# A streaming encoder step: an early end of the gating stage for tile 0, the last two chunks of the last tile alone, and conditioning pieces that wait by an account

## The chip, the core and the metric

One core of a Trainium2 chip runs the kernel. TensorE (PE in the profile) multiplies, VectorE (DVE) and ScalarE (ACT) do what is elementwise, SyncE (SP) issues the DMAs, and each engine works through its own queue in order. The metric is the device time in microseconds of one execution; the time before is the median of three.

## The reference

One step of an encoder of two layers, for a prompt of 1024 frames and 32 frames of a running stream, with shared weights. Everything is float32.

```python
for i in range(DEPTH):                                       # DEPTH = 2
    mod = silu(c) @ w_ada[i] + b_ada[i]                      # 1024 x 6144, c one vector per request group
    sh1, sc1, gt1, sh2, sc2, gt2 = split(mod, 6)
    h = rmsnorm(x, g_norm[i, 0]) * (1 + sc1) + sh1
    mix = sgu_mixer(h, ...) if i == 0 else pool_mixer(h, ...)
    x = x + gt1 * rmsnorm(mix, g_norm[i, 1])
    h = rmsnorm(x, g_norm[i, 2]) * (1 + sc2) + sh2
    f = square(relu(h @ ffn_w_up[i])) @ ffn_w_down[i]        # 1024 x 4096, 4096 x 1024
    x = x + gt2 * rmsnorm(f, g_norm[i, 3])

def sgu_mixer(h, ...):
    u, v = split(gelu(h @ w_in), 2)                          # 1024 x 4096
    v = rmsnorm(v, g_v)
    s[g] = (w_s[g] * mask) @ v[chunk, g] + b_s[g]            # 8 groups of 256 channels, chunks of 128 frames
    return (u * s) @ w_out, v                                # 2048 x 1024
```

The outputs are x of both requests, the normalised v rows of the stream, and the last 15 rows that the pooling mixer saw.

## The kernel before

**Tiles.** The 1056 frames lie along the free dimension in three tiles: 384, 384, and 288 (256 of the prompt and the 32 of the stream). The channels lie on the partitions, as 8 blocks of 128. Each tile has an accumulator `acc[t]` in SBUF.

**Products.** A product in float32 is made of three in the fast format: high part by high, low by high, and high by low (lines 771 to 773; 798 to 800 for v). Activations are split once, and each 512 KB piece of a weight is split when it arrives: ACT copies its high part (`wh`, line 367), DVE subtracts it for the low one (`wl`).

**The stream.** All weights come in one list, `stream`, in the order in which they are to be used: the weights of the gating stage ("v", "u", "o"), of the channel MLP ("up", "dn"), and between them the pieces of the conditioning matrix `w_ada` ("ada"), put in by `some_ada(n)`. Loads are issued on SP in this order, as many as there are slots, and consumed in this order by `stream_step`. `weave` calls it after every group of products; `need_w` and `need_ada` call it until the wanted item has been reached, so whatever stands ahead of it in the list is worked off at that point.

**Conditioning.** A column block of `w_ada` comes in two loads. `do_ada` multiplies it by the conditioning vector on DVE, 16 operations into the one buffer `aa`. A fold on PE then sums over the partitions (`ada`, line 453, 8 small products). Every fourth block, ACT copies the sums to `adas`, and a transpose on PE (`adat`, line 469) and a few DVE operations make `mod` and `coef` of them. Folds are put in the list `deferred`, and `run_deferred` runs all of them at the next step.

**Order of the work.** `sgu_item(gs, t, ...)` does two groups of the gating stage for one tile: four u products with gelu, two gates (`psp`), and, behind the next item's first product, the output product `po`. The loop goes over the pairs of groups (0,1), (2,3), (4,5), (6,7), and in each over the three tiles. With the last pair, `Stat` sums the squares of a tile (`sq_rs_t`), and `mix_to_ffn` for that tile goes into `fillers`: norm (`pn_rs`), residual, second norm (`r1_0_t`), and the MLP's operand `hh`, `hl`. The MLP of a layer goes by `passes`: (layer, chunk of 512 hidden channels, tiles). In layer 0, chunks 0, 1 and 4 to 7 take the tiles one by one, each with its own load of the weights, and chunks 2 and 3 all three at once. In layer 1 it is chunks 0 to 3 one by one and 4 to 7 with all three.

`time` is an account that is kept while the program is built: an estimate of how far PE and DVE have come. `weave` pulls steps of `fillers` while the account of DVE is behind that of PE.

**The end.** For the last tile, the last norm is taken row by row: the accumulator is scaled (`scale_last`) and transposed (`turn_last`, line 1146) while the last product still runs. `last` sums the squares by 6 small products (`pn_last`), takes the reciprocal root `r_last`, and 6 DVE operations (`xlast`) make the rows that go out. The other tiles go out by `residual`, 24 transposes (`yT`, line 1405), copies on ACT and one store per 128 frames (line 1407). Tile 1's 24 stand behind the last product of the program.

Of the kernel before, what the change touches and what calls it, by code (L numbers as in the profile page):

```python
# [9 lines left out]
F32 = mybir.dt.float32  # L10
# [24 lines left out]
def tile_stream_encoder_step(  # L35
# [87 lines left out]
    eps1 = const.tile([P, 1], F32, name="eps1")  # L123
    nc.vector.memset(eps1, EPS)
# [125 lines left out]
    def w_groups(gs):  # L250
        for g in gs:
            for k in range(2):
                f = 2 * g + k
                add_w(
                    ("u", g, k),
# [3 lines left out]
        for q in range(2):  # L259
            for g in gs:  # L260
                add_w(
                    ("o", g, q),
# [31 lines left out]
    passes += [(1, c, every) for c in range(4, 8)]  # L294
# [26 lines left out]
    groups = [(g, g + 1) for g in range(0, 8, 2)]  # L321
    for i, gs in enumerate(groups):
        w_groups(gs)
        if i < 3:
            some_ada((6, 8, 8)[i])
    wide = [n for n, (l, _, tiles) in enumerate(passes) if len(tiles) > 1]
    for n in range(len(passes)):
        w_chunk(n)
        if n in wide:
            some_ada(12 if passes[n][0] == 0 else 2)  # L330
# [7 lines left out]
    state = {"issued": 0, "next": 0, "raw": 0}  # L338
# [55 lines left out]
    def do_ada_pe(l, sl, q, r):  # L394
# [31 lines left out]
        deferred.append(fold)  # L426


    def do_ada(l, sl, q, r):
# [16 lines left out]
        def fold():  # L446
# [29 lines left out]
            deferred.append(fold2)  # L476

        deferred.append(fold)

    def run_deferred():  # L480
        for _ in range(len(deferred)):
            deferred.pop(0)()
# [34 lines left out]
    def stream_step():  # L517
# [4 lines left out]
        run_deferred()  # L522
# [11 lines left out]

    def need_w(key):
        while key not in witem:
            assert stream_ready(), key
            stream_step()
        return witem[key]

    def need_ada(l, which):
# [4 lines left out]
        run_deferred()  # L546
        run_deferred()
# [37 lines left out]
    def weave(streams=1):  # L585
        if streams:
            n = 0
            run_deferred()
            while n < streams and stream_ready():
                stream_step()  # L590
                n += 1
# [30 lines left out]
    class Stat:  # L622

        def __init__(self, t, tag, split=True):
            self.t, self.tag, self.n, self.split = t, tag, ncol[t], split

        def square(self, k, src=None):
# [11 lines left out]
            if w == 1:  # L641
                for j in [k - 1] if k < 7 else [6, 7]:
                    if j > 0:
# [314 lines left out]
    def sgu_item(gs, t, mix, after):  # L958
# [26 lines left out]
        def up(g, k):  # L985
# [3 lines left out]
            products(ps, n, up_terms(("u", g, k), t))  # L989
            if t == NT - 1:  # L990
                w_finish(("u", g, k))
# [53 lines left out]
        def down():  # L1045
            for d in range(KB):
                ps = ps_dn(f"po{gs[0]}_{t}_{d}")
                terms = []
                for j, (a, b) in enumerate(hid):
                    wh, wl = need_w(("o", gs[j // 2], d // 4))  # L1050
# [8 lines left out]
                if t == NT - 1 and d % 4 == 3:  # L1059
                    for g in gs:  # L1060
                        w_finish(("o", g, d // 4))
# [13 lines left out]
    def ffn_item(p, t, after):  # L1075
# [17 lines left out]
        def down():  # L1093
            for d in range(KB):
# [11 lines left out]
                if after is not None:  # L1106
                    st.square(d)
                    if l == 1 and t == NT - 1:
                        scale_last(d)
                        if d > 0:  # L1110
# [65 lines left out]
    for gs in groups:  # L1176
        mix = {g: sgu_group(g) for g in gs}
        for t in range(NT):
            sgu_item(gs, t, mix, to_ffn0 if gs == groups[-1] else None)
# [166 lines left out]
    def to_out(st):  # L1346
# [8 lines left out]
        def last():  # L1355

            turn_last(KB - 1)
# [101 lines left out]
```

## Time and profile before

| what | us |
| --- | --- |
| time, median of 3 runs | 2229.41 (2227.93 to 2232.3) |
| the profiled execution | 2227.71 |
| its span | 2225.9 |
| PE busy | 2191.3 (98%) |
| DVE busy | 1370.2 (62%) |
| ACT busy | 950.1 (43%) |
| mean granted clock of PE | 0.995 |

The span is the time between the first and the last recorded instruction. Matmuls are pipelined, so the duration of one is longer than the distance to the next. The granted clock is the share of PE's full speed that the throttle allowed in a stretch.

### The profile page before, as it was taken

The page shows a single profiled execution, that of the slowest core. Times are in us where ns is not written, and L with a number is a line of the kernel's source. Part 1 is how long each engine was busy: PE and PEld are TensorE (multiplying, and loading weights), DVE is VectorE, ACT ScalarE, POOL GpSimd, SP SyncE. Part 2 cuts the span into 40 slices and gives each one's busy share as a digit, 9 for nine tenths or more (in the row PEclk, how much of TensorE's full clock was granted, in tenths as well). Part 3 has the DMA queues.
Part 4 walks back from the last instruction along what each step waited for, and adds up shares of the span by engine and source line. Part 5 has one row for each costly group of instructions (what it writes and reads, how often), then busy time and mean ns, then how long its engine had stood idle before and what let it go on. Part 6 is the DMA issues. An engine that isn't in the chain of part 4 may idle for free.

```text
span 2225.9 us, 33634 instructions
## 1 busy us (share of the span) xinstructions
PE 2191.3 (98%) x13478; PEld 2096.9 (94%) x13478; DVE 1370.2 (62%) x2609; ACT 950.1 (43%) x1641; POOL 0.7 (0%) x6
## 2 busy tenths in 40 slices
PE   7999999999999999999999999999999999999998
PEld 4777899999998999999999999999999999999998
DVE  4855746575478856675447878878775553424355
ACT  4633422112256654223435556666564542312334
POOL 0000000000000000000000000000000000000000
PEclk9999999999999999999999999999999999999999
DMA  8465624233145544333444556655454541202112
GB/s 291 158 220 166 194 73 136 84 123 94 56 137 157 175 140 142 95 123 114 131 130 136 167 156 192 189 186 159 144 172 128 159 152 48 86 15 81 57 51 94
DMA packets 344897, 295.67 MB, mean 133 GB/s; under 512 B 10179, under 2 KB 322955, under 8 KB 344741
## 3 DMA queue, kind: packets, MB, share of 16 engines
q1 hardware_dynamic: 344468, 293.43, 42.3%
q8 instruction: 105, 1.72, 0.3%
q14 instruction: 52, 0.42, 0.1%
q10 hardware_dynamic: 272, 0.10, 0.0%
HBM read 261.65 MB, written 31.84 MB: 132 GB/s over the span
## 4 chain that ended last, share of the span: by engine, by line
PE 86%; DMA 1%; ACT 0%; DVE 0%; issue 0%; DVEq 0%; SPq 0%; ACTq 0%
PE pf L771 11%; PE pf L772 11%; PE pf L773 11%; PE pg L771 11%; PE pg L772 11%; PE pg L773 11%; PE po L771 3%; PE po L772 3%; PE po L773 3%; PE pu L771 2%; PE pu L773 2%; PE pu L772 2%; PE psp L1005 1%; PE pp L1322 1%; PE ada L453 0%; PE yT L1405 0%
## 5 line engine op out<-in xcount | busy, mean ns | idle before, releaser
L771 PE MATMUL pf<-hh,wh_up 128*128 128x384 f32 (+1 forms) x1536 | 497.8, 325 | 2.2 <-ACT hh L745 1.8
L771 PE MATMUL pg<-fh,wh_dn 128*128 128x384 f32 (+1 forms) x1536 | 498.4, 325 | 0.0
L772 PE MATMUL pf<-hl,wh_up 128*128 128x384 f32 (+1 forms) x1536 | 496.5, 324 | 0.0
L773 PE MATMUL pf<-hh,wl_up 128*128 128x384 f32 (+1 forms) x1536 | 495.3, 323 | 0.0
L772 PE MATMUL pg<-fl,wh_dn 128*128 128x384 f32 (+1 forms) x1536 | 494.8, 322 | 0.0
L773 PE MATMUL pg<-fh,wl_dn 128*128 128x384 f32 (+1 forms) x1536 | 493.9, 322 | 0.0
L771 PEld LDWEIGHTS pf<-hh,wh_up 128*128 128x128 f32 x1536 | 288.6, 188 | 5.7 <-ACT hh L745 2.2
L771 PEld LDWEIGHTS pg<-fh,wh_dn 128*128 128x128 f32 x1536 | 288.5, 188 | 2.9 <-issue 1.2
L772 PEld LDWEIGHTS pf<-hl,wh_up 128*128 128x128 f32 x1536 | 288.7, 188 | 1.2 <-DVE hl L79 0.7
L772 PEld LDWEIGHTS pg<-fl,wh_dn 128*128 128x128 f32 x1536 | 288.6, 188 | 0.8
L773 PEld LDWEIGHTS pg<-fh,wl_dn 128*128 128x128 f32 x1536 | 288.7, 188 | 0.0
L773 PEld LDWEIGHTS pf<-hh,wl_up 128*128 128x128 f32 x1536 | 288.7, 188 | 0.0
L79 DVE TENSOR_TENSOR wl_up<-raw,wh_up 128x1024 fp32r<-128x1024 f32 x144 | 176.1, 1223 | 167.3 <-ACT wh_up L367 167.0
L367 ACT ACTIVATE wh_up<-raw 128x1024 fp32r<-128x1024 f32 x144 | 152.7, 1060 | 286.0 <-PE pf L772 233.4
L79 DVE TENSOR_TENSOR acc<-acc,pg 128x384 f32<-128x384 f32 (+1 forms) x336 | 173.7, 517 | 159.9 <-PE pg L773 159.3
L367 ACT ACTIVATE wh_dn<-raw 128x1024 fp32r<-128x1024 f32 x144 | 152.5, 1060 | 202.7 <-PE pg L772 169.4
L79 DVE SCALAR_TENSOR_TENSOR aa<-raw,csil,aa 128x256 f32<-128x256 f32 x560 | 231.0, 477 | 1.9 <-DMA raw<-in_w_ada_dram 1.9
L79 DVE TENSOR_TENSOR wl_dn<-raw,wh_dn 128x1024 fp32r<-128x1024 f32 x144 | 176.0, 1223 | 81.7 <-ACT wh_dn L367 81.6
L1087 ACT ACTIVATE r<-pf 128x384 f32<-128x384 f32 (+1 forms) x192 | 86.6, 452 | 216.3 <-PE pf L773 211.5
L79 DVE TENSOR_TENSOR fl<-r,fh 128x384 fp32r<-128x384 f32 (+1 forms) x192 | 100.2, 522 | 117.0 <-ACT fh L925 115.4
L771 PE MATMUL pu<-hh,wh_u 128*128 128x384 f32 (+1 forms) x384 | 126.5, 329 | 0.0
L773 PE MATMUL pu<-hh,wl_u 128*128 128x384 f32 (+1 forms) x384 | 124.5, 324 | 0.0
(254 smaller groups left out, 2881.5 us busy)
## 6 DMA issues: line engine op xcount, KB each, us to landing
raw<-in_ffn_w_up_dram SPq DMA_DIRECT2D x144, 512.0 KB, 4.1
raw<-in_ffn_w_down_dram SPq DMA_DIRECT2D x144, 512.0 KB, 3.4
raw<-in_w_ada_dram SPq DMA_DIRECT2D x96, 512.0 KB, 3.9
raw<-in_sgu_w_in_dram SPq DMA_DIRECT2D x32, 512.0 KB, 4.6
xd<-acc SPq DMA_DIRECT2D x8, 1536.0 KB, 7.2
xo_r<-xd SPq DMA_DIRECT2D x32, 384.0 KB, 4.0
vd<-vt SPq DMA_DIRECT2D x32, 256.0 KB, 2.9
raw<-in_sgu_w_out_dram SPq DMA_DIRECT2D x16, 512.0 KB, 3.9
```

What stands on the lines that cost most here:

```text
L79: return op(out, *args, **kw)
L367: act(out=wh, in_=r, func=AF.Copy)
L771: mm(ps[:, :n], wh, rh, start=i == 0, stop=False)
L772: mm(ps[:, :n], wh, rl, start=False, stop=False)
L773: mm(ps[:, :n], wl, rh, start=False, stop=i == last)
L1005: mm(sp[:, c * P : (c + 1) * P], vl[:, c, k * P : (k + 1) * P], wr[:, c * P : (c + 1) * P], start=True, stop=True,)
L1087: act(out=r[:, :n], in_=ps[:, :n], func=AF.Relu)
L1322: mm(ps[:, :n], wg[:, k, e * P : (e + 1) * P], A(t, 2 * g + k), start=k == 0, stop=k == 1)
```

## The change

Three things are changed, and some arithmetic at the end.

- The gating stage goes over `mixes`: the pairs (0,1) and (2,3) for all tiles, (4,5) and (6,7) for tile 0 alone, then (4,5) and (6,7) for tiles 1 and 2. The weights and the spatial matrices of groups 4 to 7 are loaded, split and transposed twice. The numbers of conditioning pieces between the weights are changed with it.
- In layer 1, chunks 6 and 7 run for tiles 0 and 1, and after that for tile 2 alone, with loads and splits of their own.
- `stream_waits` holds `weave` back from the next item of the stream: a weight, if it is more than five ahead of the last one used and DVE's account is over 1 us ahead of PE's; a conditioning piece, if DVE's account is over 0.5 us ahead, or if the fold before it hasn't run. A deferred step can have a time on PE's account before which it isn't run: 0.3 us after the chain for a fold, 0.8 us after the copy for its transpose. `need_w` and `need_ada` go on as before.
- At the end, epsilon is added with the first addition of squares. The sum over the channel blocks is finished by PE, which adds the last block's squares to those of the other seven; `ms_last` is gone. `turn_last` goes two blocks at a time.

```diff
@@ -120,8 +120,6 @@
-    eps1 = const.tile([P, 1], F32, name="eps1")
-    nc.vector.memset(eps1, EPS)
@@ -247,19 +245,20 @@
         for q in range(4):
             add_w(*v_item(p, q))
 
-    def w_groups(gs):
+    def w_groups(n):
+        gs, _ = mixes[n]
         for g in gs:
             for k in range(2):
                 f = 2 * g + k
                 add_w(
-                    ("u", g, k),
+                    ("u", n, g, k),
                     sgu_w_in[0][:, f * P : (f + 1) * P].rearrange("(k p) f -> p k f", p=P),
                     (8, P),
                 )
         for q in range(2):
             for g in gs:
                 add_w(
-                    ("o", g, q),
+                    ("o", n, g, q),
                     sgu_w_out[0][g * 256 : (g + 1) * 256, q * 512 : (q + 1) * 512].rearrange(
                         "(k p) d -> p k d", p=P
                     ),
@@ -291,7 +290,10 @@
     passes += [(0, c, every) for c in range(2, 4)]
     passes += [(0, c, [t]) for t in every for c in range(4, 8)]
     passes += [(1, c, [t]) for t in every for c in range(4)]
-    passes += [(1, c, every) for c in range(4, 8)]
+    passes += [(1, c, every) for c in range(4, 6)]
+
+    passes += [(1, c, every[:-1]) for c in (6, 7)]
+    passes += [(1, c, [NT - 1]) for c in (6, 7)]
 
     rest = []
 
@@ -318,16 +320,19 @@
         w_vpiece(p)
         some_ada(8)
     rest += [(1, j) for j in (*range(8, 16), *range(8), *range(16, 48))]
-    groups = [(g, g + 1) for g in range(0, 8, 2)]
-    for i, gs in enumerate(groups):
-        w_groups(gs)
-        if i < 3:
-            some_ada((6, 8, 8)[i])
-    wide = [n for n, (l, _, tiles) in enumerate(passes) if len(tiles) > 1]
-    for n in range(len(passes)):
+
+    mixes = [((0, 1), every), ((2, 3), every), ((4, 5), every[:1]), ((6, 7), every[:1])]
+    mixes += [((4, 5), every[1:]), ((6, 7), every[1:])]
+    for n in range(len(mixes)):
+        w_groups(n)
+        if n < 2:
+            some_ada((6, 8)[n])
+    for n, (l, c, tiles) in enumerate(passes):
         w_chunk(n)
-        if n in wide:
-            some_ada(12 if passes[n][0] == 0 else 2)
+        if l == 0:
+            some_ada(12 if len(tiles) > 1 else 4 if c in (4, 5) and tiles == every[:1] else 0)
+        elif len(tiles) > 1:
+            some_ada(4)
     some_ada(99)
 
     worder = [s[1] for s in stream if s[0] == "w"]
@@ -335,7 +340,7 @@
     wdone = set()
     raws = {}
     loads = {}
-    state = {"issued": 0, "next": 0, "raw": 0}
+    state = {"issued": 0, "next": 0, "raw": 0, "used": 0}
     deferred = []
 
     def in_raw(k):
@@ -423,7 +428,7 @@
             )
             ada_finish(l, sl, red.rearrange("p (s h m) -> p s h m", s=1, h=2))
 
-        deferred.append(fold)
+        defer(fold)
 
 
     def do_ada(l, sl, q, r):
@@ -473,13 +478,20 @@
                     pb[:, :P].rearrange("p (v h m) -> p m h v", v=NV, h=2)[:, 0:4],
                 )
 
-            deferred.append(fold2)
-
-        deferred.append(fold)
-
-    def run_deferred():
-        for _ in range(len(deferred)):
-            deferred.pop(0)()
+            defer(fold2, 0.8)
+
+        defer(fold, 0.3)
+
+    def defer(step, us=None):
+
+        at = 0.0 if us is None else max(time["pe"], time["dve"]) + us
+        deferred.append((at, step))
+
+    def run_deferred(force=False):
+        n = len(deferred)
+        while n > 0 and (force or deferred[0][0] <= time["pe"]):
+            deferred.pop(0)[1]()
+            n -= 1
 
     junk = room("l", NT - 1, "xsq")
 
@@ -519,7 +531,7 @@
         k = state["next"]
         kind, key, ap, shape = stream[k]
         issue()
-        run_deferred()
+        run_deferred(force=kind == "ada" and key[2] == 0)
         r = raws.pop(k)
         if kind == "w":
             do_w(key, r)
@@ -532,7 +544,17 @@
             state["raw"] -= 1
         issue()
 
+    def stream_waits():
+
+        kind, key = stream[state["next"]][:2]
+        if kind == "w":
+            return bool(fillers) and wpos[key] > state["used"] + 5 and time["dve"] > time["pe"] + 1.0
+        if kind == "ada" and deferred and key[2] == 0:
+            return True
+        return kind == "ada" and time["dve"] > time["pe"] + 0.5
+
     def need_w(key):
+        state["used"] = max(state["used"], wpos[key])
         while key not in witem:
             assert stream_ready(), key
             stream_step()
@@ -543,8 +565,8 @@
         while state["next"] <= k:
             assert stream_ready()
             stream_step()
-        run_deferred()
-        run_deferred()
+        run_deferred(True)
+        run_deferred(True)
 
     def w_finish(key):
         wdone.add(key)
@@ -586,7 +608,7 @@
         if streams:
             n = 0
             run_deferred()
-            while n < streams and stream_ready():
+            while n < streams and stream_ready() and not stream_waits():
                 stream_step()
                 n += 1
         while time["dve"] < time["pe"] and fillers:
@@ -639,8 +662,17 @@
             )
 
             if w == 1:
-                for j in [k - 1] if k < 7 else [6, 7]:
-                    if j > 0:
+                for j in [k - 1] if k < 7 else [6, 7] if self.split else [6]:
+                    if j == 1 and not self.split:
+                        stt(
+                            out=sq[:, 0, :],
+                            in0=sq[:, 0, :],
+                            scalar=epsT,
+                            in1=sq[:, j, :],
+                            op0=ALU.add,
+                            op1=ALU.add,
+                        )
+                    elif j > 0:
                         tt(out=sq[:, 0, :], in0=sq[:, 0, :], in1=sq[:, j, :], op=ALU.add)
             else:
                 for j in [k - 2] if k < 6 else [4, 6]:
@@ -955,7 +987,9 @@
         nc.vector.memset(wt[64:P, 0:64], 0.0)
         return wt, bb
 
-    def sgu_item(gs, t, mix, after):
+    def sgu_item(p, t, mix, after):
+        gs, tiles = mixes[p]
+        last = t == tiles[-1]
         n = ncol[t]
         col0, npr, nsm = TILES[t]
         nch = npr // P
@@ -986,9 +1020,9 @@
             if k == 0:
                 inputs(g)
             ps = ps_up(f"pu{g}_{t}_{k}")
-            products(ps, n, up_terms(("u", g, k), t))
-            if t == NT - 1:
-                w_finish(("u", g, k))
+            products(ps, n, up_terms(("u", p, g, k), t))
+            if last:
+                w_finish(("u", p, g, k))
             u = t_m(f"u{g}_{t}_{k}")
             act(out=u[:, :n], in_=ps[:, :n], func=AF.Gelu_apprx_tanh)
             us.append(u)
@@ -1047,7 +1081,7 @@
                 ps = ps_dn(f"po{gs[0]}_{t}_{d}")
                 terms = []
                 for j, (a, b) in enumerate(hid):
-                    wh, wl = need_w(("o", gs[j // 2], d // 4))
+                    wh, wl = need_w(("o", p, gs[j // 2], d // 4))
                     o = (j % 2) * 512 + (d % 4) * P
                     terms.append((wh[:, o : o + P], wl[:, o : o + P], a[:, :n], b[:, :n]))
                 products(ps, n, terms)
@@ -1056,9 +1090,9 @@
                     st = Stat(t, f"rs_{t}")
                 if after is not None:
                     st.square(d)
-                if t == NT - 1 and d % 4 == 3:
+                if last and d % 4 == 3:
                     for g in gs:
-                        w_finish(("o", g, d // 4))
+                        w_finish(("o", p, g, d // 4))
                 weave(d % 2)
             if after is not None:
                 after(st)
@@ -1107,7 +1141,8 @@
                     st.square(d)
                     if l == 1 and t == NT - 1:
                         scale_last(d)
-                        if d > 0:
+                        if d in (2, 4, 6):
+                            turn_last(d - 2)
                             turn_last(d - 1)
                 if last and d % 2 == 1:
                     w_finish(("dn", p, d // 2))
@@ -1173,10 +1208,10 @@
     def to_ffn0(st):
         fillers.append((f"ffn0_{st.t}", mix_to_ffn(st, 0)))
 
-    for gs in groups:
+    for p, (gs, tiles) in enumerate(mixes):
         mix = {g: sgu_group(g) for g in gs}
-        for t in range(NT):
-            sgu_item(gs, t, mix, to_ffn0 if gs == groups[-1] else None)
+        for t in tiles:
+            sgu_item(p, t, mix, to_ffn0 if gs[-1] == 7 else None)
 
     sgu_stack.close()
     late = pool("late")
@@ -1354,23 +1389,26 @@
 
         def last():
 
-            turn_last(KB - 1)
+            turn_last(KB - 2)
             pn = ps_dn("pn_last")
             nb = len(LAST)
-            for i, (c0, _, _) in enumerate(LAST):
-                mm(
-                    pn[:, 2 * i : 2 * i + 2],
-                    st.sq[:, 0, c0 : c0 + P],
-                    ones[:, 0:2],
-                    start=True,
-                    stop=True,
-                )
+            for k in (0, KB - 1):
+                if k > 0:
+                    turn_last(KB - 1)
+                for i, (c0, _, _) in enumerate(LAST):
+                    mm(
+                        pn[:, 2 * i : 2 * i + 2],
+                        st.sq[:, k, c0 : c0 + P],
+                        ones[:, 0:2],
+                        start=k == 0 and i == 0,
+                        stop=k > 0 and i == nb - 1,
+                        skip_group_check=True,
+                    )
             sums = pn[:, : 2 * nb].rearrange("p (b c) -> p b c", c=2)[:, :, 0]
-            ms, r, q = (t_st(f"{x}_last")[:, :nb] for x in ("ms", "r", "q"))
-            act(out=r, in_=sums, func=AF.Abs_reciprocal_sqrt, bias=eps1, scale=1.0 / D)
-            ts(ms, sums, 1.0 / D, EPS, op0=ALU.mult, op1=ALU.add)
+            r, q = (t_st(f"{x}_last")[:, :nb] for x in ("r", "q"))
+            act(out=r, in_=sums, func=AF.Abs_reciprocal_sqrt, scale=1.0 / D)
             tt(out=q, in0=r, in1=r, op=ALU.mult)
-            stt(out=q, in0=q, scalar=-0.5, in1=ms, op0=ALU.mult, op1=ALU.mult)
+            stt(out=q, in0=sums, scalar=-0.5 / D, in1=q, op0=ALU.mult, op1=ALU.mult)
             stt(out=r, in0=q, scalar=1.5, in1=r, op0=ALU.add, op1=ALU.mult)
             xt = last_ps["x"]
             dsts = [dst for _, _, dst in blocks]
```

## The prediction

> **What bounds the kernel now.** I read the page's totals first, then who TensorE waits for, then the granted clock in windows round those waits.
>
> ```profile
> span 2225.9 us, 33634 instructions
> PE 2191.3 (98%) x13478; PEld 2096.9 (94%) x13478; DVE 1370.2 (62%) x2609; ACT 950.1 (43%) x1641; POOL 0.7 (0%) x6
> ```
> ```profile
> PE pn_rs L671 <- ACT sc_rs L656: 3.8, 1, 3.8
> PE psp L1005 <- DMA vl<-vd: 2.7, 1, 2.7
> PE yT L1405 <- DVE xlast L79: 2.1, 1, 2.1
> PE pf L771 <- ACT hh L745: 1.8, 1, 1.8
> PE wsT L952 <- DMA ws<-in_sgu_w_s_dram: 1.6, 2, 1.1
> PE adat L469 <- ACT adas L465: 1.6, 2, 1.1
> PE pn_last L1361 <- DVE sq_rf L79: 1.2, 1, 1.2
> PE pv L799 <- DVE wl_v L79: 0.3, 1, 0.3
> ```
> ```profile
> 273.00:278.00 5.00, 2.27 (x23) 1.78 (x22) 3.63 (x10) 0.00 (x0) 0.00 (x0) 1.00 0.81 262
> 671.10:677.90 6.80, 5.01 (x13) 3.98 (x14) 6.71 (x13) 3.41 (x7) 0.00 (x0) 0.50 0.49 135
> 2209.95:2213.90 3.95, 1.51 (x12) 1.03 (x10) 2.12 (x7) 1.43 (x4) 0.00 (x0) 1.00 0.00 0
> 2213.90:2218.00 4.10, 2.60 (x11) 2.20 (x12) 3.50 (x6) 0.93 (x2) 0.00 (x0) 0.50 0.69 256
> ```
> TensorE is busy for 98% of the span, so the mathematics is fixed and 2225.9 - 2191.3 = 34.6 us of idle time is all there is to move, with the time lost to a lowered clock on top. Rows of the second view are: who waits for what, us in total, times, longest. The third gives window, length, busy us of PE, PEld, DVE, ACT, POOL, then the granted clock. Two places stand out in the body of the run. At the start of the first channel MLP (667 to 678 us) PE waits 3.8 us for tile sums and 1.8 us for the first operand, and then runs 6.8 us at clock 0.50. At the end, 2209.95 is where the last product stops and the span still has 2225.9 - 2209.95 = 15.95 us to go.
>
> The profiled execution took 2227.71 us, 1.70 less than the median 2229.41; I sum changes against the profiled one and add them to the median.
>
> **1. Tile 0 leaves the gating stage early.** Pairs (4,5) and (6,7) now run for tile 0 first, with their own weights, then again for tiles 1 and 2. In the changed program's order tile 0's sums (pn_rs_0, instruction 2833 of PE; its second norm at 3065) stand some 400 to 600 instructions ahead of its first MLP product (3451); before they stand at 3226 and 3474 against 3564. The 3.8 + 1.8 us of waiting goes. The half clock costs half of the busy part of 6.8 us: 5.01 x 0.5 = 2.5, and 0.6 of small gaps beside (an estimate); **-8.7**. Next late is tile 1's handover in the MLP: the work of VectorE between its sums and its operand stands against about 36 us of products, with 1.4 to 2.6 us to spare; 0, with +2 as the other end.
>
> Added with it: 32 weight splits with their 512 KB loads (16 here, 16 in part 4), two table loads on ACT, 4 more transposes of the spatial matrices.
>
> ```profile
> L79 DVE TENSOR_TENSOR wl_u<-raw,wh_u 128x1024 fp32r<-128x1024 f32 x16 | 19.5, 1219 | 6.8 <-ACT wh_u L367 6.8
> L367 ACT ACTIVATE wh_u<-raw 128x1024 fp32r<-128x1024 f32 x16 | 16.9, 1058 | 57.6 <-PE pu L772 53.3 <-DMA raw<-in_sgu_w_in_dram 4.3
> 246.00:667.00 421.00, 416.68 (x2704) 407.18 (x2697) 260.75 (x591) 117.95 (x204) 0.00 (x0) 1.00 0.36 111
> 1900.00:2205.00 305.00, 304.93 (x1948) 302.65 (x1948) 131.96 (x239) 98.37 (x182) 0.00 (x0) 1.00 0.20 61
> L952 PE MATMUL wsT<-ident,ws 128*128 128x128 f32 x8 | 2.5, 310 | 1.6 <-DMA ws<-in_sgu_w_s_dram 1.6
> ```
> Sixteen splits are 16 x 1.22 = 19.5 us of VectorE and 16 x 1.06 = 17 of ACT in a stage of 421 us where they are busy 261 and 118; in the last 305 us they are busy 132 and 98. Both have room, so 0 (if that cover were gone, see the fourth rival). The transposes are on PE: 4 x 0.31 = 1.2, and their matrices come by DMA through one buffer: 1.6 us was waited for in 8, so 0.8 in 4. **+2.0**, bounds 1.2 and 4.4 (each waiting 0.8, half of the 1.6 that two waited).
>
> **2. Pieces of conditioning wait for an account.** A piece is a chain on VectorE into one buffer, and the fold on PE that reads the buffer frees it for the next:
>
> ```profile
> 121.48 0.42 PE L453 MATMUL ada<-aa,pick 128*32 128x128 f32 x8
> 121.97 0.62 DVE L79 TENSOR_SCALAR aa<-raw,csil 128x256 f32<-128x256 f32 x2 [4.81 <-PE ada L453]
> 110.41 0.62 DVE L79 TENSOR_SCALAR aa<-raw,csil 128x256 f32<-128x256 f32 x2 [3.67 <-PE ada L453]
> 110.94 0.67 DVE L79 TENSOR_TENSOR vt<-vt,pv 32x512 f32<-32x512 f32 x1
> 111.54 5.62 DVE L79 SCALAR_TENSOR_TENSOR aa<-raw,csil,aa 128x256 f32<-128x256 f32 x14
> 124.52 0.17 DVE L79 TENSOR_TENSOR mod<-adat,vec 128x16 f32<-128x16 f32 x1 [1.14 <-PE adat L469]
> 125.00 0.24 DVE L79 SCALAR_TENSOR_TENSOR coef<-mod,vec 128x8 f32<-128x8 f32 x2
> 118.41 0.39 PE L800 MATMUL pv<-wh_v,hl 128*128 128x512 f32 x1
> 118.64 0.39 PE L798 MATMUL pv<-wh_v,hh 128*128 128x512 f32 x1
> ```
> The chain begins 0.49 us after its fold begins and takes 111.54 + 5.62 - 110.41 = 6.75 us, a vt addition included. A v product is issued every 118.64 - 118.41 = 0.23 us. Before, the fold stood about 40 such products (9.2 us) ahead of the third v piece. In the changed order it stands 16 ahead: the account holds pieces back, and the third and the fourth v piece (PE instructions 599 and 824) then force them, since weights and pieces are consumed in one fixed order. Count from the start of that fold: PE does the fold, 0.4; 16 products, 3.7; one transpose, 0.3; two products, 0.5; it stands still at 4.9. VectorE ends the chain at 0.49 + 6.75, adds mod and coef, 0.17 + 2 x 0.24 = 0.65, and so 7.9; only then comes the split of the weight PE wants, 1.22 (as wl_u): 9.1. PE meanwhile does two short folds and one product. About **4.0 us of standing, twice**, less 0.3 that the pv row had: **+7.7**. Behind these waits in PE's queue is the whole v stage and nothing else fills. The lower bound is 0 (the forced pieces are ready after all), the upper 2 x 5, if the raw load, which waits for a slot that the chain frees, is late as well.
>
> The start of the gating stage takes the same form: the first u weight's load waits for the piece before it to leave its slot, so I reckon 2.55 us for a piece and 1.2 us for a split, 4.0 with what lies between. What it replaces is the 2.7 us wait for vl, whose load now stands ahead of the state's loads on SP's queue, and some 0.6 about it: **+0.7**, bounds -3.3 and +2.
>
> The transpose of a finished block waits by the account instead of being issued at once behind the ACT copy that feeds it; its waits in the second view go: **-1.6**, at worst 0.
>
> **3. Turn of the last tile, arithmetic of the end.**
>
> ```profile
> 2209.95 0.45 DVE L79 TENSOR_TENSOR acc<-acc,pg 128x288 f32<-128x288 f32 x1 [0.50 <-PE pg L773]
> 2210.91 0.46 DVE L79 TENSOR_TENSOR sq_rf<-sq_rf 128x288 f32<-128x288 f32 x1 [0.51 <-ACT sq_rf L635]
> 2211.43 0.83 PE L1361 MATMUL pn_last<-ones,sq_rf 128*128 128x2 f32 x6 [1.19 <-DVE sq_rf L79]
> 2212.29 0.26 ACT L1370 ACTIVATE r_last<-pn_last,eps 128x3 f32<-128x3 f32 x1 [0.66 <-PE pn_last L1361]
> 2212.59 0.16 DVE L79 TENSOR_SCALAR ms_last<-pn_last 128x3 f32<-128x3 f32 x1 [1.22 <-ACT r_last L1370]
> 2213.24 2.73 DVE L79 SCALAR_TENSOR_TENSOR xlast<-yT,r_last,xlast 128x512 f32<-128x512 f32 x4
> 2216.00 1.43 DVE L79 SCALAR_TENSOR_TENSOR xlast<-yT,r_last,xlast 32x512 f32<-32x512 f32 x2
> 2216.51 4.45 PE L1405 MATMUL yT<-ident,acc 128*128 128x128 f32 x20 [0.69 <-ACT yo L1406]
> 2218.29 3.66 SPq L1407 DMA_DIRECT2D out_dram<-yo  x3
> 2222.04 1.18 SPq L1389 DMA_DIRECT2D out_dram<-xlast  x2
> 2150.00:2182.00 32.00, 3.08 (x24) 2.63 (x24) 0.00 (x0) 3.14 (x6) 1.00 0.30 95
> ```
> The last addition of squares (0.46) and the operation ms_last (0.16) go, with what lies between 0.67 less, so xlast ends at 2209.95 + 6.8 instead of 2217.43. Six stores follow on SP. Today the last two (2222.04, 1.18) sit behind tile 1's stores and land by 2225.9, 2.7 after their issue. In the changed order nothing of tile 1 is behind the last product: the last issue follows xlast's end and the landing 2.7 later, with some 0.5 for an issue: 6.8 + 0.5 + 2.7 = 10.0 against 15.95: **-5.9**.
>
> **4. Chunks 6 and 7 for the last tile alone** are what makes that possible: tiles 0 and 1 finish first, and tile 1's 24 output transposes move in front of the last product. Tile 0's, in mid-stream, kept PE 3.08 us (last row above): **+3.1**. Weights of the two chunks load twice (part 1's cover). Their stores, moved past too, find SP idle.
>
> Sum: -8.7 + 2.0 + 7.7 + 0.7 - 1.6 - 5.9 + 3.1 = **-2.7 us**, with the clock at 1.00 in the new waits: 2229.41 - 2.7 = 2226.7. About 0.2% (4.5 us: 2224.95 to 2233.87) is what a measurement of this kernel can tell from no change.
>
> **The clock** is what I can't settle. A stand of 2.7 us at 274 left it at 1.00; one of 3.8 us halved it; and so did 2209.95 to 2213.90, where PE was idle 2.44 of 3.95 us in pieces. The new stands, 4.0 us in two or three pieces, lie between. The Trainium skill ("TensorE: Matmul & The Clock Gate", section "HAM oscillation — how this bites in real kernels") says to keep PE's gaps under about 3.4 us; by that rule gaps of 2.5 us would cost nothing more and the sum stays -2.7. The tail's row agrees with it only in part: no gap there was longer than 2.1 us, and the clock still went to 0.50.
>
> **Rivals.**
> (a) *The new stands halve the clock.* Each then costs 6.8 us at half rate, less about 1.6 of it idle anyway: 2.6. It decides once PE idles over about 60% of a stretch of 3.4 us (tail: 2.44/3.95 = 62%); a stand of 2.5 + 1 us reaches that in most positions. Three places: -2.7 + 7.8 = +5.1, 2234.5, slower; one place: 2229.3. For it: the tail. Against: 274 us. 0.24 (0.14 slower, 0.10 the same).
> (b) *The forced pieces cost nothing*, because PE comes later to that point than I count. -2.7 - 7.7 = -10.4: 2219.0. For it: VectorE idles 4.8 us before the chain in the row at 121.97, waiting for PE, so spare time exists. 0.25, faster.
> (c) *The edit doesn't do what it says:* tile 1's or tile 2's sums at the end of the gating stage take the place of tile 0's, as no product is left to cover them. Then part 1's 8.7 stay: +6, 2235.4. Against: all of tile 0's first chunks lie behind them. 0.05.
> (d) *Weights of the narrow passes are late.* Every load of 512 KB serves one or two tiles where it served three. Four mixes each waiting one ACT and one VectorE split, 1.06 + 1.22 = 2.3: +9.1 to 2235.8. Against: ACT and VectorE at 28% and 62% of the stage. 0.08.
>
> **Numbers.** The forecast, 2226.7, has 0.38 (2222 to 2231 with its bounds: 0.11 of it faster, 0.27 the same). Faster: 0.11 + 0.25 = 0.36; the same 0.27 + 0.10 = 0.37; slower 0.14 + 0.05 + 0.08 = 0.27. Cases of several kinds hold the chance, so the range goes from (b), 2218.5, to the upper three, 2235.5.
>
> **What would show it.** In the profile after: no wait of pn_rs or of hh near 667; waits of PE for aa and wl_v of 2 to 3 us before pv2 and pv3, with the clock at 1.00 there (0.50 is rival a; no wait is b); no store of tile 1 behind the last product, and 10 us from it to the end; waits for wh_u, wl_u, wh_o or wl_o would be d. A granted clock under 0.95 outside the start and the end, or a tail longer than 12 us, would make the forecast wrong.

## The result, and the profile after

The changed kernel takes 2221.01 us (median of 6, 2220.15 to 2222.18) against 2229.42 us for the kernel before on the same chip: ratio 0.9962, interval 0.9949 to 0.9975. It is 8.4 us faster. The forecast was a gain of 2.7 us, to 2226.7, with 2218.5 to 2235.5 as its range.

The page's totals and PE's waits in the profile after (who waits for what, us in total, times, longest; those of the first 70 us and those under 0.5 us are left out):

```profile
span 2218.8 us, 33828 instructions
PE 2187.9 (99%) x13488; PEld 2096.6 (94%) x13488; DVE 1404.1 (63%) x2646; ACT 986.4 (44%) x1675; POOL 0.7 (0%) x6
PE ada L458 <- DVE aa L79: 5.0, 3, 2.3
PE pv L831 <- DVE wl_v L79: 1.3, 3, 0.5
PE wsT L984 <- DMA ws<-in_sgu_w_s_dram: 1.1, 2, 0.5
PE pu L805 <- DVE wl_u L79: 0.8, 1, 0.8
PE pf L805 <- DVE wl_up L79: 0.6, 1, 0.6
PE pf L803 <- ACT wh_up L372: 0.6, 1, 0.6
```

The waits for pn_rs, hh, vl, xlast and pn_last are no longer in the list. New in it are the waits for conditioning pieces (`ada` for `aa`) and small ones for weights. DVE and ACT are busy 34 and 36 us longer, beside PE. The timeline round the first new stand, and windows round both (length, busy us of PE, PEld, DVE, ACT, POOL, then the granted clock):

```profile
137.94 3.65 DVE L79 SCALAR_TENSOR_TENSOR aa<-raw,csil,aa 128x256 f32<-128x256 f32 x9
141.07 0.71 PE L830 MATMUL pv<-wh_v,hh 128*128 128x512 f32 x2
144.05 0.48 PE L458 MATMUL ada<-aa,pick 128*32 128x128 f32 x4 [2.27 <-DVE aa L79]
145.75 0.80 PE L831 MATMUL pv<-wl_v,hh 128*128 128x512 f32 x1
148.11 0.40 PE L831 MATMUL pv<-wl_v,hh 128*128 128x512 f32 x1
```
```profile
141.00:144.00 3.00, 0.78 (x4) 0.30 (x2) 3.00 (x11) 1.87 (x4) 0.00 (x0) 1.00 0.59 175
144.00:148.00 4.00, 3.95 (x15) 2.46 (x16) 2.66 (x3) 1.11 (x2) 0.00 (x0) 0.57 0.61 190
199.00:203.00 4.00, 3.05 (x17) 2.07 (x18) 3.22 (x5) 1.75 (x4) 0.00 (x0) 1.00 0.54 161
660.00:690.00 30.00, 30.00 (x197) 30.00 (x196) 28.13 (x45) 22.86 (x37) 0.00 (x0) 1.00 0.59 179
```

PE stands 2.27 us before the third v piece, and runs at half clock until 147.7. The stand before the fourth (2.19 us, up to 199.7) left the clock alone. Where the kernel before stood at 667 us, PE now is busy in all of 30 us. The end:

```profile
2209.17 0.45 DVE L79 TENSOR_TENSOR acc<-acc,pg 128x288 f32<-128x288 f32 x1 [0.80 <-PE pg L805]
2209.30 1.69 PE L1399 MATMUL pn_last<-ones,sq_rf 128*128 128x2 f32 x12
2211.02 0.17 ACT L1409 ACTIVATE r_last<-pn_last 128x3 f32<-128x3 f32 x1 [0.17 <-PE pn_last L1399]
2211.89 4.19 DVE L79 SCALAR_TENSOR_TENSOR xlast<-yT,r_last,xlast 128x512 f32<-128x512 f32 x6
2212.67 3.77 SPq L1427 DMA_DIRECT2D out_dram<-xlast  x6
```

No store of tile 1 stands between the stores of the last rows, and the span ends 2218.8 - 2209.17 = 9.6 us after the last product (counted from the start of its addition, as in the kernel before), where it was 15.95.

The time by stretches, from the starts of first instructions in the timelines (us; "v" from the first `pv` product to the first `pu`, "gating and MLP" from there to the first `pp` product of the pooling mixer, "rest" to the last addition of `pg`, "end" to the end of the span):

| kernel | to first pv | v | gating and MLP | rest | end |
| --- | --- | --- | --- | --- | --- |
| before | 25.3 | 221.0 | 1040.7 | 923.0 | 16.0 |
| after | 24.3 | 227.3 | 1031.6 | 926.0 | 9.6 |
| no_account | 25.1 | 221.2 | 1034.9 | 925.9 | 9.6 |
| no_account_2 | 24.0 | 219.7 | 1032.1 | 925.9 | 9.5 |
| mix_only | 24.2 | 222.9 | 1032.1 | 923.0 | 15.6 |
| tail_only | 24.1 | 223.4 | 1043.3 | 925.7 | 9.5 |
| account_only | 22.9 | 227.7 | 1032.8 | 930.1 | 15.6 |
| best | 24.0 | 219.3 | 1029.8 | 926.1 | 9.9 |

Each row is a single execution: the first three columns vary by 1 to 4 us between programs that are the same there; "rest" and "end" repeat within 0.4 us. The profiled execution can lie off its kernel's median: 3.6 us above it in no_account, 5.1 us below it in pieces_free. (In account_only the first pooling product is issued earlier against the rest, so its third and fourth columns are to be added: 1962.9, where before has 1963.7.)

### The profile page after: what moved, and what is told of

The parts are those of the page before. It is cut to its first block, busy times and chain, and to the rows that moved or that the text cites. A ratio compares the mean times of both kernels' runs of the same rounds, so it can differ in the third digit from the quotient of the medians.

```text
span 2218.8 us, 33828 instructions
## 1 busy us (share of the span) xinstructions
PE 2187.9 (99%) x13488; PEld 2096.6 (94%) x13488; DVE 1404.1 (63%) x2646; ACT 986.4 (44%) x1675; POOL 0.7 (0%) x6
## 4 chain that ended last, share of the span: by engine, by line
PE 92%; DVE 3%; DMA 3%; ACT 1%; issue 0%; SPq 0%; DVEq 0%; ACTq 0%
PE pf L803 11%; PE pf L804 11%; PE pf L805 11%; PE pg L803 11%; PE pg L804 11%; PE pg L805 11%; PE po L803 3%; PE po L804 3%; PE po L805 3%; PE pu L803 3%; PE pu L805 3%; PE pu L804 3%; PE pv L830 2%; PE pv L831 2%; PE pv L832 2%; DVE aa L79 2%
## 5 line engine op out<-in xcount | busy, mean ns | idle before, releaser
L79 DVE TENSOR_TENSOR wl_up<-raw,wh_up 128x1024 fp32r<-128x1024 f32 x152 | 185.8, 1223 | 169.8 <-ACT wh_up L372 169.8
L372 ACT ACTIVATE wh_up<-raw 128x1024 fp32r<-128x1024 f32 x152 | 161.0, 1059 | 281.5 <-PE pf L804 208.1
L372 ACT ACTIVATE wh_dn<-raw 128x1024 fp32r<-128x1024 f32 x152 | 161.0, 1060 | 210.6 <-PE pg L804 164.3
L79 DVE TENSOR_TENSOR wl_dn<-raw,wh_dn 128x1024 fp32r<-128x1024 f32 x152 | 185.9, 1223 | 89.3 <-ACT wh_dn L372 89.0
```

Of the source, the lines that this page charges most:

```text
L79: return op(out, *args, **kw)
L372: act(out=wh, in_=r, func=AF.Copy)
```

## The experiments

**The account taken out.**

```diff
-        at = 0.0 if us is None else max(time["pe"], time["dve"]) + us
+        at = 0.0
...
-            while n < streams and stream_ready() and not stream_waits():
+            while n < streams and stream_ready():
```

> The changed kernel with the account taken out: nothing is held back from the stream, and every deferred step runs at the next one, as before. Theory A (the account only costs: its two stands before the third and fourth v piece, 2.27 and 2.19 us with small ones behind them and one stretch at half clock, make the 6.5 us that the stretch from 100 to 250 us lost): these waits are gone, folds stand 40 products ahead again, and the time is 2221.0 - 6 = 2215 us (2213 to 2217). Theory B (the account is what keeps VectorE free for tile 0's handover to the channel MLP): the v stage gets its 6 us back, but waits for pn_rs, hh or pn_r1 come back round 560 to 680 us, and the time is 2219 to 2225 us.

Measured: 2214.93 us, ratio to the kernel before 0.9939 (0.9927 to 0.9952). Theory A's number; that it agrees to 0.1 us is chance, as the five executions lie between 2213.9 and 2218.5. Nothing came back at 560 to 680 us. PE's longest waits in the body are these:

```profile
PE psp L1039 <- DMA vl<-vd: 3.1, 1, 3.1
PE adat L474 <- ACT adas L470: 1.4, 2, 0.9
PE pf L803 <- ACT wh_up L372: 1.0, 1, 1.0
```

So the wait for vl, which the changed kernel no longer had, is back with the old order of the stream, and the v stage (221.2 us) has lost its stands.

**Tile 0's early end alone** (the kernel before, with `mixes` and the numbers of pieces).

> The kernel before, with tile 0's early end of the gating stage alone (and the numbers of conditioning pieces that go with it). Theory A (each part acts in its own place): the waits for pn_rs and hh at 667 us and the half clock behind them go, 9.7 us, and about 1 us comes for the transposes and their loads: 2229.4 - 8.7 = 2220.7 us (2219 to 2222.5). Theory B (needs the account): less than 5 us faster, with waits of PE for DVE in the handover.

Measured: 2219.83 us, ratio 0.9959 (0.9946 to 0.9971), 9.25 us below the 2229.08 of the kernel before on that chip. Theory A. This part alone gains about as much as the whole change (the two intervals overlap). The handover shows no wait, at full clock:

```profile
660.00:690.00 30.00, 30.00 (x191) 30.00 (x190) 29.38 (x47) 22.12 (x38) 0.00 (x0) 1.00 0.66 202
```

**The end alone** (chunks 6 and 7, and the arithmetic).

> The kernel before, with the last tile's chunks 6 and 7 alone and the arithmetic of the end. Theory A: the end after the last product falls from 15.95 to about 9.7 us (-6.3), tile 1's 24 output transposes stand ahead of it (+2.7): 2229.4 - 3.6 = 2225.8 us (2224.5 to 2227). Rival: the transposes cost nothing in front either, since the wait they replace is of PE and not of the copies, -6.3: 2223.1 us; or the doubled loads of two chunks make PE wait for wh_up or wl_up, 1 us each, and nothing is gained.

Measured: 2225.78 us, ratio 0.9987 (0.9978 to 0.9996), -3.3. The end fell to 9.5 us and "rest" grew from 923.0 to 925.7: both terms as expected.

**The account alone.**

> The kernel before, with the account alone. Theory A: the two stands before the third and the fourth v piece as in the changed kernel, 2.2 us each and 1 us of small ones, with half clock behind one or both: +5 to +8, less 1.6 for the transposes that no longer wait and less up to 2.7 if the wait for vl at 274 us goes with the later folds: 2229.4 + 5 = 2234 us (2231 to 2237). Theory B (the account helps the handover at 667 us by itself): 2229 us or less, with the wait for pn_rs under 2 us.

Measured: 2232.78 us, ratio 1.0017 (1.0008 to 1.0026), +3.7: Theory A.

```profile
PE ada L453 <- DVE aa L79: 5.0, 3, 2.3
PE pn_rs L688 <- ACT sc_rs L673: 3.8, 1, 3.8
```

The v stage is 6.7 us longer than in the kernel before, the wait for vl is gone, and the wait for pn_rs at 670 us is 3.76 as before: the account does nothing for the handover. The three parts alone add up to -9.25 - 3.3 + 3.7 = -8.9; together they gave -8.4.

**The two halves of the end.** Arithmetic alone, then the chunks alone:

> The kernel before with the arithmetic of the end alone (epsilon in the first addition, the last block's squares added by PE, no ms_last, turns two at a time); tile 1's transposes and stores still follow the last product. The sums are ready 0.67 us earlier and all behind them moves by that: 2229.1 - 0.7 = 2228.4 us. Rival: the end is set by tile 1's copies and stores on SP, which don't wait for xlast: 2229.1 us. Both lie within what a run can tell; the end after the last product in the trace decides (15.95 us before; 15.3 or 15.95).

> The kernel before with chunks 6 and 7 of layer 1 for tiles 0 and 1 first and then for the last tile alone, the arithmetic of the end as before. Nothing of tile 1 follows the last product, so the end after it falls from 15.95 to about 10.4 us (9.65 of the changed kernel and 0.7); tile 1's 24 transposes stand ahead, +2.7: 2229.1 - 5.6 + 2.7 = 2226.2 us (2225 to 2227.5). Rival (the arithmetic makes most of the gain): 2228.5 us or more.

Measured on one chip, where the kernel before took 2231.48: 2230.38 (ratio 0.9995, 0.9986 to 1.0004) and 2228.64 (0.9987, 0.9978 to 0.9996). The first can't be told from no change by its time; in its trace the end is 2229.85 - 2214.39 = 15.45 us, half a microsecond shorter. With the chunks it is 10.1 us, and "rest" 925.9. By its time in microseconds the second run would fall to the rival (2228.5 or more), but the kernel before was 2.4 us slower here too: the difference, 2.8 us, is the 2.9 that was expected, and the trace shows where it comes from.

**Which rule of the account makes the stands.**

```diff
-        if kind == "ada" and deferred and key[2] == 0:
-            return True
-        return kind == "ada" and time["dve"] > time["pe"] + 0.5
+        return False
```

> The changed kernel with one rule of the account taken out: conditioning pieces are no longer held back from the stream; weights are still held, and deferred steps keep their times. If the held pieces make the two stands in the v stage: those are gone and the time is that of the kernel without the account, 2215 us (2213.5 to 2216.5). If it is the times of the folds and transposes that make them late: the stands stay and it is 2220 to 2222 us.

Measured: 2219.23 us, ratio 0.9944 (0.9932 to 0.9957), on the chip that was 2.4 us slower for the kernel before. In absolute time it lies in neither interval. Its ratio is near that of the kernel without the account (0.9939), but its interval also overlaps that of the changed kernel, so the trace decides (of the fastest of its five executions, 2214.13 us). The v stage is 220.8 us with no stand before the third and fourth piece: holding pieces back makes them, not the times of the folds.

**A version with three more waits taken away, which failed.** The stream's v rows are written later, the transpose of a finished block waits (the next piece forces the folds only), and eight pieces move (against the changed kernel; the new body of `run_deferred` is not shown):

```diff
-        if n < 2:
-            some_ada((6, 8)[n])
+        some_ada((6, 8, 0, 0, 4, 4)[n])
...
-            some_ada(12 if len(tiles) > 1 else 4 if c in (4, 5) and tiles == every[:1] else 0)
+            some_ada(12 if len(tiles) > 1 else 0)
...
-        at = 0.0 if us is None else max(time["pe"], time["dve"]) + us
-        deferred.append((at, step))
+        at = time["pe"] + 2.5 if us == 0.8 else 0.0
+        deferred.append((at, step, us == 0.8))
...
-        run_deferred(force=kind == "ada" and key[2] == 0)
+        run_deferred("folds")
...
-            while n < streams and stream_ready() and not stream_waits():
+            while n < streams and stream_ready():
...
-            yield False
+            yield 10.0
-    fillers.append(("state", sgu_state()))
...
+        if p == 1:
+            fillers.append(("state", sgu_state()))
```

> The changed kernel without the account, and with three waits taken away that its trace still shows: the steps that write out the v rows of the stream begin with the second pair of groups and 10 us apart, so that their DMAs don't stand ahead of vl on SP (3.1 us at 274); the eight conditioning pieces of layer 0's chunks 4 and 5 go to the gating pairs of tiles 1 and 2 (wh_up and wl_up, 1.6 us and a stretch at half clock at 1095); the transpose of a finished block comes 2.5 us of PE's account later and is not forced by the next piece (0.9 and 0.5 us at 123 and 238). If each wait is worth what it shows: 2214.9 - 3.1 - 3.0 - 1.4 = 2207.4 us (2206 to 2210). Rival: moved pieces and stores make new waits in the gating stage, and it stays at 2213 to 2216.

Measured: 2228.94 us, ratio 0.9993 (0.9984 to 1.0002): the gain is lost, which neither expectation allowed for. The three waits are gone from the trace, and these stand in it, with half clock behind them:

```profile
PE pn_rs L702 <- ACT sc_rs L687: 4.1, 1, 4.1
PE pf L802 <- ACT hh L776: 3.7, 2, 2.0
PE pn_r_2x L702 <- DVE sm_r_2x L79: 2.2, 1, 2.2
```

Tile 0's handover is late again: its second norm (`pn_r_0x`) comes at 653.7 us, 17 us ahead of the first MLP product, where the changed kernel has it at 593.8, 62 us ahead. From the program, the eight pieces in the pairs of tiles 1 and 2 keep the account of VectorE ahead of PE's there, so `weave` doesn't pull the handover; the account itself is in no trace, so this step is argued. Tile 0's early end alone is not enough: as the run best shows below, the eight pieces must not stand behind it.

**That told apart, and the changed kernel beside it on one chip.** First the changed kernel and the one without the account, again:

> The changed kernel as it is, on the same chip as the three below. Its ratio to the kernel before was 0.9962; the same is expected, and its profile should show whether a stand of 2.2 us before the third v piece always brings a stretch at half clock (it did at 144 us and did not at 199 us).

> The changed kernel without the account, again. Expected 5 to 6 us (ratio 0.9972 to 0.9978) below the changed kernel on this chip, as the stands in the v stage are worth; if the account is worth nothing either way, the two agree within 2 us.

Measured: 2221.03 (ratio 0.9964, 0.9951 to 0.9976) and 2214.10 us (0.9939, 0.9925 to 0.9952): the account costs 6.9 us on this chip, somewhat more than the 5 to 6 expected, and 6.1 between the earlier ones. On the clock, the changed kernel's second profile shows the reverse of the first:

```profile
144.00:148.00 4.00, 3.65 (x21) 2.61 (x18) 2.34 (x3) 1.40 (x2) 0.00 (x0) 1.00 0.71 190
199.00:203.00 4.00, 3.61 (x15) 2.45 (x16) 2.66 (x3) 1.31 (x4) 0.00 (x0) 0.72 0.60 174
```

And then the failed version without the moved pieces:

> The kernel without the account, with later steps for writing out the v rows of the stream and a later transpose of a finished block, and the conditioning pieces where the changed kernel has them. The run named hybrid moved eight pieces into the gating pairs of tiles 1 and 2 and had the waits for pn_rs and hh back. If those pieces were the reason, this one keeps the early handover (pn_rs_0 stands at PE instruction 2833 as in the changed kernel) and gains the waits for vl and adat: 3.1 + 1.4 us below the kernel without the account. If the later steps were the reason, the waits at 660 us are there again and it is some 10 us slower than that.

Measured: 2211.40 us, ratio 0.9922 (0.9908 to 0.9935). It is the fastest of all, 17.4 us below the kernel before and 9.6 below the changed one, and 2.7 below the kernel without the account where 4.5 was expected. It differs from hybrid in the place of the eight pieces alone, so they are the reason for the late handover there. The handover stays early, and PE's largest waits behind the first 70 us are these:

```profile
span 2209.0 us, 33825 instructions
PE 2183.9 (99%) x13488; PEld 2095.4 (95%) x13488; DVE 1404.1 (64%) x2646; ACT 985.7 (45%) x1675; POOL 0.7 (0%) x6
PE wsT L983 <- DMA ws<-in_sgu_w_s_dram: 2.2, 2, 1.1
PE pf L805 <- DVE wl_up L79: 0.6, 1, 0.6
PE pn_r_2x L703 <- ACT xt L1200: 0.4, 1, 0.4
```

The same with the old numbers of pieces:

```diff
-        if n < 2:
-            some_ada((6, 8)[n])
+        if n < 3:
+            some_ada((6, 8, 8)[n])
...
-            some_ada(12 if len(tiles) > 1 else 4 if c in (4, 5) and tiles == every[:1] else 0)
+            some_ada(12 if len(tiles) > 1 else 0)
```

> The same with the numbers of conditioning pieces of the kernel before (6, 8 and 8 behind the first three pairs, none in layer 0's chunks 4 and 5): eight pieces go to the pair (4,5) of tile 0. If pieces in the MLP make the wait for wh_up and wl_up at 1095 us (1.6 us and some half clock), it is 1.5 to 3 us faster than the run above. Rival: 8 x 6.75 / 2 = 27 us of VectorE in the pair that ends 35 us before tile 0's handover makes that late, and it is slower by up to 5 us with waits for pn_r1 or hh near 640 us.

Measured: 2219.02 us, ratio 0.9954 (0.9941 to 0.9966): 7.6 us slower than the run above. The rival had the sign, but not the size (up to 5 us) and not the cause. The handover was not late; the pieces themselves were. They fall into tile 0's short pair, all in a row on VectorE, and PE comes to their folds and to the weight behind them too early:

```profile
PE ada L458 <- DVE aa L79: 4.6, 2, 3.5
PE pu L803 <- ACT wh_u L372: 2.3, 1, 2.3
480.00:500.00 20.00, 12.60 (x67) 9.60 (x66) 18.79 (x47) 2.28 (x3) 0.00 (x0) 0.84 0.51 154
```

The wait at 1095 us did go, as expected. Moving these eight pieces trades it (0.6 us in the run above) for waits many times its size.

## Why the prediction was right, and what was mis-sized

The sign was right, and each of the three parts acted where I had placed it. The range held because it was wide: 2221.0 lies below the 2222 to 2231 that I gave the forecast itself, and nearer to rival (b), 2219.0, whose mechanism didn't happen. One sign that I had named for a wrong forecast was there too: the clock fell to 0.57 in the v stage.

**Tile 0's handover (-8.7).** Right in size; whose wait it was I had read wrong. These are the rows of the kernel before at the handover, and one of the kernel after:

```profile
671.14 0.61 PE L671 MATMUL pn_rs<-sc_rs,ones 128*128 128x288 f32 x1 [3.75 <-ACT sc_rs L656]
674.05 0.69 PE L771 MATMUL pf<-hh,wh_up 128*128 128x384 f32 x1 [1.75 <-ACT hh L745]
```
```profile
695.98 0.29 PE L703 MATMUL pn_rs<-sc_rs,ones 128*128 128x288 f32 x1
```

Only tile 2 has 288 columns, so the 3.75 us were spent on tile 2's sums, which stood in PE's queue right ahead of tile 0's first MLP product; tile 0's own sums had come at 614 us without a wait. In the changed kernel tile 0's operand is ready when its first MLP product starts, at 655.3 us, and tile 2's sums stand among MLP products 41 us later and wait for nothing. The waits for pn_rs and hh are gone, the clock is 1.00 there, and tile 1's handover, given 0 to +2, shows no wait. With this part alone the stretch of gating and MLP is 1040.7 - 1032.1 = 8.6 us shorter, although it holds two new waits for wh_up and wl_up at 1094 us, 1.15 us together.

**What comes with it (+2.0).** Mis-sized by nearly all of it. I priced four transposes at the duration of a row, 0.31 us; but PE's operations overlap, and tile 0's 24 transposes in 3.08 us, a row that I used for another term, had shown 0.13 us each. The matrices' loads, reckoned at +0.8, wait 1.1 us in total now, less than the 1.6 before. So this term was about +0.5 - 0.5 = 0.

**The stands in the v stage (+7.7, less 1.6).** Right in place, wrong in make-up, and the sum agrees by luck. PE arrived and stood as counted: 2.27 and 2.19 us before the fold. The second wait, 1 us for the split, was nothing at the third piece and 0.25 us at the fourth, since the second half of the fold and one product at that point take longer than I let them, 1.2 to 1.7 us. Waits of 0.7 us for the weights behind each follow some 8 us later. All these waits are 6.15 us, against 0.29 in the kernel before: +5.9 where I had 7.7. The transposes' 1.6 us went as counted. What makes up for the rest is the clock, which I had at 1.00: 1.7 us. The v stage grew by 227.3 - 221.0 = 6.3 us against 6.1 forecast; these are single executions, but the medians with and without the account differ by 6.1 and 6.9 us as well, so the whole of it goes with the account.

**The start of the gating stage (+0.7).** Wrong sign. PE waited 0.51 us for the piece and 0.79 for the weight, not 2.55 and 1.2: it came there late itself, behind a wait of 0.55 for a spatial matrix, and the vl wait of 2.7 went. That is about 0.55 + 0.51 + 0.79 - 0.49 - 2.73 = -1.4 (0.49 is the wait for that matrix before). Against the -2.7 that I forecast, the two profiled executions differ by -7.1: this term and the transposes are 2.1 + 2.0 of the 4.4 between them, the end 0.4 and the first 25 us 1.0 (they vary by that much between programs that are equal there), less what the new waits for weights cost. The medians differ by 1.3 us more, since the profiled execution of the kernel before was 1.7 below its median and the one of the changed kernel 0.4.

**The end (-5.9, +3.1).** Measured -6.3 and +3.0. The arithmetic has half a microsecond of it, the order of the work the rest.

**The clock, rival (a).** It happened, without deciding the sign. In three profiles with the account (after, account_only, changed_again), stands of 2.2 to 2.3 us halved the clock four times out of six. Each time the stretch was short: 0.57 over 4 us is 4 x 0.43 / 0.5 = 3.4 us at half, so 1.7 us, where I had taken 6.8 us and 2.6 from the row at 671, which lay behind two waits. So two places cost about 2.3 us on average, not 5.2 (nor 7.8 for three).

Rival (a)'s condition, PE idle for about 60% of a stretch of 3.4 us, fits the traces better than I had noticed. In each trace the changes of the clock lie on one grid of 3.41 us, so a stand counts by how it falls on that grid. Windows cut on the grid of the profile after, round the first stand and round the second:

```profile
140.85:144.26 3.41, 1.14 (x9) 0.55 (x7) 3.41 (x11) 2.13 (x5) 0.00 (x0) 1.00 0.54 160
144.26:147.67 3.41, 3.41 (x14) 2.03 (x11) 2.40 (x3) 0.85 (x1) 0.00 (x0) 0.50 0.61 188
195.46:198.87 3.41, 2.04 (x10) 1.03 (x8) 3.41 (x10) 1.06 (x2) 0.00 (x0) 1.00 0.46 133
198.87:202.29 3.42, 2.34 (x14) 1.48 (x15) 3.35 (x5) 1.88 (x4) 0.00 (x0) 1.00 0.46 128
```

The first stand falls into one window, and the next window is at half clock; the second is split between two, and nothing follows. Eight profiles have the wait for vl (2.5 to 3.1 us), and five show half clock behind it. In these 14 stands, PE is busy for 0.68 to 1.43 us in the window ahead of a half clock, and for 1.53 us or more in every window of theirs where none follows. The edge is not sharp: in no_account a window with 1.78 us busy, at 1094, was followed by half clock too. So what I held against rival (a), the stand at 274 us with the clock at 1.00 (1.53 us busy), was luck of one execution, and the account, which removes that wait, saves more there than the wait.

The Trainium skill's rule ("TensorE: Matmul & The Clock Gate", "HAM oscillation — how this bites in real kernels"), no gaps over about 3.4 us, doesn't hold here as a bound: gaps of 2.2 us brought half clock. The Trainium skill's free-running window of 3413 ns (the same page, "What's actually happening") agrees with the grid of 3.41 us in these traces. That one stand of one program halves the clock in one execution and not in the next fits as well.

**Rivals (b), (c), (d).** (b) is refuted in the changed kernel: the pieces bound. (c) didn't happen in it, and it is what happened in the run named hybrid, by the mechanism named (the sums of the other tiles right ahead of the first MLP product) and from a cause that I had not named, the eight pieces. It is also what the kernel before had, as the row at 671.14 shows. (d) is the 1.2 us at 1098 in this profile; in no_account the same two waits, 1.6 us, had 3.4 us at half clock behind them. The 0.8 us for wl_u belongs to the start of the gating stage.

## What to carry to other kernels

When PE is at 98%, cost an edit from the order of its queue: count the products between a producer and its consumer, and compare with the producer's chain; that gave the place of the new stands, and the size of the first wait in each, before any run. Price short PE operations at the distance between two starts, not at the duration of a row. An account that holds work back must not hold what a later step will force in one piece: here the account's gain for the handover was nil and its cost 6 to 7 us (3.7 on the kernel before, give or take 2), while where the pieces stand in the list decided between 2211 and 2229 us (0.992 and 0.999 of the kernel before). And look at the shape of a row that waits before naming its owner: 288 columns told which tile's sums these were.

## What the runs showed of the hardware that I had not expected

A stand of PE of 2.2 us, with 0.8 us of work round it in 3 us, is enough for about 3.4 us at half clock. Whether that comes changes from one execution to the next (four of six), with the place of the stand on a grid of 3.41 us whose start differs between executions. The wait for vl, 2.5 to 3.1 us, left the clock at 1.00 in the profile before and in two others, and halved it in five, as here in tail_only, behind a wait of 2.67 us:

```profile
280.00:284.00 4.00, 4.00 (x17) 4.00 (x16) 4.00 (x11) 1.69 (x4) 0.00 (x0) 0.59 0.83 257
```

0.59 over 4 us is again 3.3 us at half.

The kernel before took 2229.1, 2231.5 and 2228.8 us on three occasions, so differences of 2 us between kernels were read only from ratios on one chip.
